# The first norm of a decoder layer by tokens, x turned on TensorE, and three of sixteen blocks of each first-projection row in plain float32

## The chip, the cores and the metric

The kernel runs one decoder layer on one core of one Trainium2 chip. Its time is the device time in microseconds (us) of one launch. The profile splits that core into TensorE (PE, with its weight loads PEld), VectorE (DVE), ScalarE (ACT), GpSimd (POOL) and SyncE (SP), which issues most of the transfers.

## The reference, cut to what matters

```python
def rmsnorm(x, g):
    xf = x.astype(F32)
    y = xf * lax.rsqrt(jnp.mean(xf * xf, axis=-1, keepdims=True) + EPS)
    return (y * g.astype(F32)).astype(x.dtype)

c_act = jax.nn.silu(c)
mod = (c_act @ w_ada[l] + b_ada[l]).reshape(B, 6, 1, D)
shift1, scale1, gate1, shift2, scale2, gate2 = jnp.moveaxis(mod, 1, 0)
h = rmsnorm(x, g_norm_mix[l]) * (1.0 + scale1) + shift1
q_a, k_c, v_c, k_s, v_s, k_w, v_w, g_a, q_r, k_r, v_r, g_r = split_cols(h @ w_in[l], IN_SIZES)
... attention and retention on these, the output projection, a second norm, the PEER layer ...
```

There are 256 tokens and 2048 features; everything is float32. `w_in` has 6704 columns. The change touches the norm of `x` and the first part of `h @ w_in`.

## The kernel before, in words

**Layout.** Features lie on the 128 partitions: `xT` holds x as 16 feature blocks k of [128 features x 256 tokens]. The projection `h @ w_in` is done in stages, each a stretch of the profile. Stage A (about 20 to 90 us) takes the blocks k = 0 to 7 of h against 2048 columns of `w_in` (16 output blocks of 128), one weight chunk `winA[k]` of 128 x 2048 (1 MB) for each k; this is "row k" below. Stage C takes the same k against 1024 more columns, stage B all 16 k against 1664 columns, stage D and later stages the rest, mixed with the attention. After them come the output projection, the second norm and the PEER layer, from about 700 us to the end.

**Splitting.** A float32 product is made of three products in the faster rounded type fp32r: each weight chunk is split by `split` into `whi` (a cast on ACT, line 157, in two halves) and `wlo` (raw minus whi on DVE, line 158, in two halves), and h into `hh` and `hl` in the tile `act`. `rows_T` (line 354) then issues hi x hh, hi x hl and lo x hh for each of the 16 blocks of a row: 48 matmuls of 256 columns.

**The modulation.** Scale and shift come from `w_ada`, 1 MB for each group of 128 outputs. `ada_chunk` loads one chunk and multiplies it by the row `crow` (silu of c) on DVE with a sum over the row (line 198). Row k of stage A needs two such chunks; with them `scol` and the shift of block k are made (lines 338 and 339, DVE), and `modulate` (lines 295 to 297) scales `xT[:, k]` in place on ACT, casts it to `hh` on ACT and subtracts to `hl` on DVE.

**The first norm before.** `xT` is loaded already turned by the host. Sixteen squares on ACT are added up by sixteen steps on DVE; `row_rstd` sums over partitions on PE, takes the power -0.5 on POOL, spreads the result over the partitions with one more matmul, and `normalise` multiplies all of `xT` by it on DVE (line 300).

**Buffers and queues.** Raw chunks (weights, w_ada, at the start also c) share a ring of four buffers `raw`; a load is issued on SP in the program's order as soon as the buffer's last reader is done, so a load that waits holds back all that stand behind it. Slot for slot, the chunk `winA[k]` hands its buffer to the first w_ada chunk of row k + 2. Each engine works through its own list in order; a scheduler that plans with its own model of times writes these lists when the program is built, so an edit can change the order of instructions that it doesn't name. `whi` and `wlo` have two buffers each. The eight PSUM banks go by the tags S, T, O and A, two each.

## Time and profile before

| what | value |
|---|---|
| three timed runs | 1860.74 us median, 1860.2 to 1863.67 us |
| profiled execution | 1856.91 us |
| its span, first to last instruction | 1855.2 us, mean granted clock 0.99 |
| busy share of the span | PE 97%, DVE 80%, ACT 38%, POOL 20% |
| HBM | 350 GB/s over the span |

The profiled execution's own time is 1.7 us above its span and 3.8 us below the median of the timed runs. A row of the timeline has the start, the duration, the engine, the line of the code, the operation, output and inputs, the shapes, the count, and in brackets how long the engine stood idle before it and what ended that. A row of the windows has the stretch and its length, then for each engine the busy time and the number of instructions, then the granted TensorE clock, the busy share of the DMA engines and the rate in GB/s. In the chain of waits a row has the start, the duration and what the end of the program hung on there.

### The profile page before, as it was taken

The numbers are of one execution on the slowest core, as the hardware profiler recorded it, in microseconds if no ns is written. First come the engines' busy times: TensorE is split into PE (matmuls) and PEld (weight loads), VectorE is DVE, ScalarE is ACT, GpSimd is POOL, SyncE is SP. The second block draws the span as 40 slices with busy tenths as digits, with TensorE's granted clock in tenths as the row PEclk, the third lists the DMA queues.
The fourth block names the chain that finished last, engine by engine and source line by source line (L and its number), as shares of the span: only waits on it lengthen the run. The fifth ranks groups of instructions, "written<-read, shape, count | busy, mean of one in ns | idle before, by whom it ended". The sixth has DMA issues, their size and how long they took to land.

```text
span 1855.2 us, 28510 instructions
## 1 busy us (share of the span) xinstructions
PE 1793.1 (97%) x11264; PEld 1571.5 (85%) x11264; DVE 1485.7 (80%) x2336; ACT 708.7 (38%) x1284; POOL 366.1 (20%) x259
## 2 busy tenths in 40 slices
PE   5899999999889999999999999999999999999997
PEld 4899878797767899999997777779999998777775
DVE  7988889889779999586498999983555558998878
ACT  3444453745435421021045555541111114555554
POOL 1000001011010012211124434420111114544210
PEclk9999899999999999999999999999999999999999
DMA  8989887889887799999889999989999989999992
GB/s 341 409 320 362 313 308 292 342 302 334 318 338 279 278 322 364 424 366 376 332 346 386 423 420 416 409 355 425 367 345 359 354 316 404 426 421 403 388 316 99
DMA packets 94616, 653.96 MB, mean 353 GB/s; under 512 B 11409, under 2 KB 11633, under 8 KB 18449
## 3 DMA queue, kind: packets, MB, share of 16 engines
q1 hardware_dynamic: 66818, 467.78, 65.2%
q0 software_dynamic: 27664, 184.37, 25.3%
q8 instruction: 88, 1.44, 0.3%
q14 instruction: 46, 0.38, 0.1%
HBM read 644.97 MB, written 4.22 MB: 350 GB/s over the span
## 4 chain that ended last, share of the span: by engine, by line
PE 87%; DVE 7%; DMA 3%; issue 1%; ACT 1%; POOL 0%; SPq 0%; ACTq 0%; POOLq 0%; DVEq 0%
PE acc L990 31%; PE psU L1111 28%; PE psN L453 8%; PE psD L354 4%; PE psA L237 3%; PE bkB L354 2%; DMA raw<-in_adaT 2%; PE psA L238 1%; PE pg L1096 1%; DVE raw L198 1%; DVE wlo L158 1%; PE bkC L354 1%; PE bvB L406 1%; DMA raw<-in_winA 1%; PE pT L552 1%
## 5 line engine op out<-in xcount | busy, mean ns | idle before, releaser
L1111 PE MATMUL psU<-xT,raw 128*128 128x160 f32 x4096 | 569.5, 300 | 0.0
L1111 PEld LDWEIGHTS psU<-xT,raw 128*128 128x128 f32 x4096 | 558.3, 190 | 0.4
L990 PE MATMUL acc<-whi,cc 128*128 128x512 f32 x1512 | 369.1, 391 | 0.0
L990 PEld LDWEIGHTS acc<-whi,cc 128*128 128x128 f32 x1512 | 283.8, 188 | 70.0 <-issue 1.5
L967 DVE TENSOR_TENSOR wlo<-raw,whi 128x2048 fp32r<-128x2048 f32 x126 | 288.1, 2287 | 55.1 <-issue 47.4
L990 PE MATMUL acc<-wlo,cc 128*128 128x512 f32 x1008 | 254.2, 392 | 0.8 <-DVE wlo L967 0.6
L964 ACT CAST whi<-raw 128x2048 fp32r<-128x2048 f32 x126 | 240.7, 1911 | 0.5 <-DMA raw<-in_v 0.5
L198 DVE SCALAR_TENSOR_TENSOR raw<-raw,crow 128x2048 f32<-128x2048 f32 x96 | 219.0, 2283 | 19.7 <-DMA raw<-in_adaT 19.6
L157 ACT CAST whi<-raw 128x1024 fp32r<-128x1024 f32 (+1 forms) x174 | 168.5, 1018 | 167.1 <-DMA raw<-in_winA 32.4
L158 DVE TENSOR_TENSOR wlo<-raw,whi 128x1024 fp32r<-128x1024 f32 (+1 forms) x174 | 200.6, 1181 | 24.2 <-ACT whi L157 23.8
L990 PEld LDWEIGHTS acc<-wlo,cc 128*128 128x128 f32 x1008 | 161.5, 161 | 63.8 <-DVE wlo L967 3.1
L453 PE MATMUL psN<-whi,act 128*128 128x512 f32 x512 | 166.9, 402 | 1.4 <-ACT act L677 0.7
L1117 DVE TENSOR_TENSOR X<-X,ge 128x160 f32<-128x160 f32 (+19 forms) x94 | 25.8, 276 | 162.7 <-ACT ge L1116 160.5
L1113 ACT ACTIVATE X<-psU 128x160 f32<-128x160 f32 (+19 forms) x102 | 25.6, 251 | 315.6 <-PE psU L1111 299.6
L453 PEld LDWEIGHTS psN<-whi,act 128*128 128x128 f32 x512 | 95.9, 189 | 25.6 <-issue 1.7
L453 PE MATMUL psN<-wlo,act 128*128 128x512 f32 x256 | 103.3, 404 | 3.4 <-DVE wlo L158 3.4
L953 ACT CAST cc<-X 128x192 fp32r<-128x192 f32 x126 | 44.0, 352 | 148.1 <-PE acc L990 147.5
L237 PE MATMUL psA<-act,whi 128*128 128x512 f32 x240 | 87.2, 404 | 3.8 <-ACT whi L157 3.8
L806 POOL DMA_INDIRECT rows<-in_urow,sx x32 | 67.1, 2097 | 105.3 <-DVE rows L847 100.4
L806 POOL DMA_INDIRECT s<-in_urow,sx x26 | 53.9, 2072 | 120.6 <-DVE s L847 86.5
L354 PE MATMUL psD<-act,whi 128*128 128x256 f32 x384 | 75.4, 294 | 0.6 <-ACT whi L157 0.6
L969 ACT CAST cc<-cc 128x64 fp32r<-128x64 f32 x126 | 30.4, 243 | 117.2 <-DVE cc L954 117.2
(363 smaller groups left out, 2551.0 us busy)
## 6 DMA issues: line engine op xcount, KB each, us to landing
raw<-in_u SPq DMA_DIRECT2D x128, 1024.0 KB
raw<-in_v SPq DMA_DIRECT2D x128, 1024.0 KB
raw<-in_adaT SPq DMA_DIRECT2D x96, 1024.0 KB
raw<-in_winN SPq DMA_DIRECT2D x16, 1024.0 KB
raw<-in_woutN SPq DMA_DIRECT2D x16, 1024.0 KB
raw<-in_wqT SPq DMA_DIRECT2D x16, 1024.0 KB
raw<-in_winB SPq DMA_DIRECT2D x16, 832.0 KB
raw<-in_winD SPq DMA_DIRECT2D x12, 1024.0 KB
```

The source lines that it names most:

```text
L157: nc.scalar.copy(hi[:, sl], r[:, sl])
L158: nc.vector.tensor_sub(lo[:, sl], r[:, sl], hi[:, sl].bitcast(F32))
L198: nc.vector.scalar_tensor_tensor(r, r, 1.0, crow, op0=OP.mult, op1=OP.mult, accum_out=modc[:, j, k:k + 1])
L237: nc.tensor.matmul(p_, hi[:, sl], act[:, k], start=k == 0, stop=False, skip_group_check=True)
L354: nc.tensor.matmul(bank[:, b, :], x[:, w], y[:, k, :], start=k == k0 and n == 0 and first, stop=k == k1 - 1 and n == 2, skip_group_check=True)
L453: nc.tensor.matmul(ps[tt], x[:, k, ts_], y[:, w], start=k == 0 and j == 0, stop=k == KB - 1 and j == 2)
L806: pin(nc.gpsimd.indirect_dma_start(out=r, out_offset=None, in_=src, in_offset=bass.IndirectOffsetOnAxis(ap=o, axis=0)))
L953: inorder(nc.scalar.copy(ch, xb(j)))
L964: inorder(nc.scalar.copy(hi, r))
L967: nc.vector.tensor_sub(lo[:, i:i + n], r[:, i:i + n], hi[:, i:i + n].bitcast(F32))
L990: return nc.tensor.matmul(acc[c][0:m], x, w[:, c[1] * 512:(c[1] + 1) * 512], start=jj == 0 and n == 0, stop=jj == HALF - 1 and n == 2 - c[ ...
L1111: nc.tensor.matmul(ps, w[:, k * P:(k + 1) * P], xT[:, k, 0:TU], start=k == 0, stop=k == KB - 1)
```

## The change

x is loaded by tokens, `xt` = [128 tokens, 2 halves, 2048], in four pieces. Four squares on ACT, each with its own sum over 1024 features, give the sums of squares directly (`ss0`); `token_rstd` makes the factor of each token (DVE, the power on POOL). The factors are put on the diagonal of two matrices (`dg00` and `dg01`), and 32 float32 matmuls of `xt` against them turn and scale x at once; each matmul is two records in the trace. ACT copies the results from eight PSUM banks to `xT`, 512 columns a time. `sumsq`, `row_rstd`, `normalise` and the host's turned copy of x go away.

In stage A the first NF = 3 of the 16 blocks of a row are multiplied in plain float32, straight from the raw chunk against the modulated `xT`; only the other 1664 columns are split. The raw buffer is thus read by PE too.

Lastly, the first four loads of `nal` (the distance penalties of the attention, on POOL's queue) now wait for a one-column copy from `gT`, which is made at the end of stage B; before, they were issued in the first microseconds.

```diff
-    o["xT"] = g["x"].reshape(S, KB, P).transpose(2, 1, 0)
...
-        for q in range(4):
-            nc.sync.dma_start(xT[:, 4 * q:4 * q + 4, :], a["xT"][:, 4 * q:4 * q + 4, :])
+        xt = fp.tile([P, 2, D], F32, name="xt", tag="oT")
+        for tt in range(2):
+            for h in range(2):
+                nc.sync.dma_start(xt[:, tt, h * 1024:(h + 1) * 1024], a["x"][:, tt, h * 1024:(h + 1) * 1024])
...
-        acc = fp.tile([P, S], F32, name="sqacc")
-        for k in range(KB):
-            sumsq(fp, k, acc, xT[:, k, :])
-        rrow = row_rstd(pp, fp, [acc], ["S", "S"], ident)
-        for k in range(0, KB, 4):
-            normalise(xT[:, k:k + 4, :], xT[:, k:k + 4, :], rrow)
+        ss = fp.tile([P, 2, 2], F32, name="ss0")
+        sq = fp.tile([P, 1024], F32, name="sq0", tag="cT")
+        for tt in range(2):
+            for h in range(2):
+                nc.scalar.activation(sq, xt[:, tt, h * 1024:(h + 1) * 1024], AF.Square, accum_out=ss[:, tt, h:h + 1])
+        rc = token_rstd(fp, ss, 2, "rc0")
+        dgs = []
+        for tt in range(2):
+            dgs.append(fp.tile([P, P], F32, name=f"dg0{tt}", tag=f"ksw{tt}"))
+            nc.vector.tensor_scalar(dgs[tt], ident, rc[:, tt:tt + 1], None, op0=OP.mult)
+        for k, t in zip(range(0, KB, 2), "SSTTOOAA"):
+            ps = pp.tile([P, 2, 2, P], F32, name="psx", tag=t)
+            for i in range(2):
+                for tt in range(2):
+                    nc.tensor.matmul(ps[:, i, tt, :], xt[:, tt, (k + i) * P:(k + i + 1) * P], dgs[tt], start=True, stop=True)
+            nc.scalar.copy(xT[:, k:k + 2, :], ps.rearrange("p i t s -> p i (t s)"))
...
         for k in range(KH):
-            hi, lo = win_row(a["winA"], k, 2048)
+            r = raw_tile()
+            nc.sync.dma_start(r, a["winA"][k])
+            hi, lo = split(r[:, NF * P:], 2048 - NF * P)
             row_in(k)
             background("A")
-            for b in range(16):
-                rows_T(bk[b // 2], b % 2, hi, lo, b * P, k, 0, KH, b % 2 == 0)
+            for b in range(NF):
+                nc.tensor.matmul(bk[b // 2][:, b % 2, :], r[:, b * P:(b + 1) * P], xT[:, k, :], start=k == 0 and b % 2 == 0,
+                                 stop=k == KH - 1, skip_group_check=True)
+            for b in range(NF, 16):
+                rows_T(bk[b // 2], b % 2, hi, lo, (b - NF) * P, k, 0, KH, b % 2 == 0)
...
                     nal = fp.tile([P, 384], F32, name="nal", bufs=4)
+                    if gp == 0 and r < 2:
+                        nc.scalar.copy(nal[:, 0:1], gT[:, 0:1])
                     nc.gpsimd.dma_start(nal, a["nali"][h])
```

The order of the loads on SP in stage A is the same as before: two w_ada chunks, one `winA` chunk, and again. On ACT and DVE the order changes. Line numbers of the changed kernel are other ones: its lines 264, 265 and 266 are the lines 295, 296 and 297 of before (the modulation), 156 and 157 are 157 and 158 (the split), 197 is 198 (w_ada times c), 314 and 315 are 338 and 339, 347 and 349 are 370 and 372 (the copies of stage A's results out of PSUM, on DVE and on ACT).

On ACT, in stage A, two rows k and k + 1 read so before:

```order
L157 CAST whi<-raw 128x1024 x2
L295 ACTIVATE xT<-xT,modc,scol 128x256
L296 CAST act<-xT 128x256
L157 CAST whi<-raw 128x1024 x2
L295 ACTIVATE xT<-xT,modc,scol 128x256
L296 CAST act<-xT 128x256
```

and in the changed kernel so:

```order
L264 ACTIVATE xT<-xT,modc,scol 128x256
L156 CAST whi<-raw 128x832 x2
L265 CAST act<-xT 128x256
L264 ACTIVATE xT<-xT,modc,scol 128x256
L156 CAST whi<-raw 128x832 x2
L265 CAST act<-xT 128x256
```

The cast of a row's weight chunk stood ahead of the row's modulation (which waits for `scol`); it now stands behind it.

On DVE, in stage A of the changed kernel, one row and the head of the next read:

```order
L197 SCALAR_TENSOR_TENSOR raw,modc<-raw,crow 128x2048 x2
L314 TENSOR_TENSOR modc<-modc,cols 128x2
L315 TENSOR_SCALAR scol<-modc,cols 128x1
L157 TENSOR_TENSOR wlo<-raw,whi 128x832 x2
L266 TENSOR_TENSOR act<-xT,act 128x256
L197 SCALAR_TENSOR_TENSOR raw,modc<-raw,crow 128x2048 x2
```

`scol` is followed at once by the subtraction `wlo`, which needs the cast; before, the second subtraction (L297, `act`) stood between the two w_ada multiplies instead of ahead of them.

At the turn from stage A to stage C, ACT reads before:

```order
L372 COPY oT<-bkA_192 128x512
L372 COPY oT<-bkA_194 128x512
L157 CAST whi<-raw 128x1024 x2
L372 COPY oT<-bkA_196 128x512
L295 ACTIVATE xT<-xT,modc,scol 128x256
L372 COPY oT<-bkA_198 128x512
```

and in the changed kernel the first cast of stage C stands behind all four copies:

```order
L349 COPY oT<-bkA_187 128x512
L349 COPY oT<-bkA_189 128x512
L349 COPY oT<-bkA_191 128x512
L349 COPY oT<-bkA_193 128x512
L156 CAST whi<-raw 128x1024 x4
```

On DVE at the same turn, the changed kernel has both w_ada multiplies behind the last subtraction of stage A (L266) and ahead of stage C's first `wlo`; before, one of the two stood ahead of that subtraction:

```order
L266 TENSOR_TENSOR act<-xT,act 128x256
L197 SCALAR_TENSOR_TENSOR raw,modc<-raw,crow 128x2048
L347 COPY oT<-bkA_188 128x512
L347 COPY oT<-bkA_190 128x512
L197 SCALAR_TENSOR_TENSOR raw,modc<-raw,crow 128x2048
L347 COPY oT<-bkA_192 128x512
L347 COPY oT<-bkA_194 128x512
L314 TENSOR_TENSOR modc<-modc,cols 128x2
L157 TENSOR_TENSOR wlo<-raw,whi 128x1024
```

In the attention (from about 200 us on) the lists of PE, DVE and ACT hold the same work in partly other order.

More of the change, by code (lines that the diff above doesn't have):

```diff
@@ L247, in summed @@
         nc.vector.tensor_add(dst, dst, ps[:, 0, 0:n])
-    def sumsq(wpool, kb, acc, src, tag="pr"):
-        sq = wpool.tile([P, S], F32, name="sq", tag=tag, bufs=3)
-        nc.scalar.activation(sq, src, AF.Square)
-        if kb == 0:
-            nc.vector.tensor_copy(acc, sq)
-        else:
-            nc.vector.tensor_add(acc, acc, sq)
-    def row_rstd(pool, wpool, accs, tags, ident, copy=True):
-        ps = [pool.tile([P, 2], F32, name="psq", tag=t) for t in tags]
-        for i, acc in enumerate(accs):
-            for tt in range(2):
-                nc.tensor.matmul(ps[tt][:, 0:1], acc[:, tt * P:(tt + 1) * P], ones[:, 0:1], start=i == 0, stop=i == len(accs) - 1)
-        rc = wpool.tile([P, 2], F32, name="rcol")
-        for tt in range(2):
-            nc.vector.tensor_scalar(rc[:, tt:tt + 1], ps[tt][:, 0:1], 1.0 / D, EPS, op0=OP.mult, op1=OP.add)
-        pow_mhalf(rc, rc, 2)
-        dg = wpool.tile([P, S], F32, name="rdiag", tag="pr", bufs=3)
-        for tt in range(2):
-            nc.vector.tensor_scalar(dg[:, tt * P:(tt + 1) * P], ident, rc[:, tt:tt + 1], None, op0=OP.mult)
-        ps = pool.tile([P, S], F32, name="psr", tag=tags[0])
-        nc.tensor.matmul(ps, ones, dg, start=True, stop=True)
-        if not copy:
-            return ps
-        r = wpool.tile([P, S], F32, name="rrow")
-        nc.scalar.copy(r, ps)
-        return r
     with ExitStack() as fctx:
@@ L297, in modulate @@
             nc.vector.tensor_sub(hl[:, k:e, :], t, hh[:, k:e, :].bitcast(F32))
-        def normalise(dst, src, rrow):
-            nc.vector.tensor_mul(dst, src, rrow[:, None, :].to_broadcast([P, dst.shape[1], S]))
         kcv = fp.tile([P, 4, 2, P], F32, name="kcv", tag="f4k", bufs=2)
-        ksw = [fp.tile([P, S], F32, name=f"ksw{i}") for i in range(4)]
         vsw = fp.tile([P, 2, 512], F32, name="vsw")
         gT = fp.tile([P, S], F32, name="gT", tag="pr", bufs=3)
-        oT = fp.tile([P, KB, S], F32, name="oT")
-        cT = fp.tile([P, KB // 2, S], F32, name="cT")
         pp = fctx.enter_context(tc.tile_pool(name="fpsum", bufs=2, space=PS))
@@ L312, in body @@
         crow = c_row(fp, pp)
-        for q in range(4):
-            nc.sync.dma_start(xT[:, 4 * q:4 * q + 4, :], a["xT"][:, 4 * q:4 * q + 4, :])
+        xt = fp.tile([P, 2, D], F32, name="xt", tag="oT")
+        for tt in range(2):
+            for h in range(2):
+                nc.sync.dma_start(xt[:, tt, h * 1024:(h + 1) * 1024], a["x"][:, tt, h * 1024:(h + 1) * 1024])
         rowc = dram.tile([1, D], F32, name="rowc")
         nc.gpsimd.dma_start(rowc, crow[0:1, :])
-        acc = fp.tile([P, S], F32, name="sqacc")
-        for k in range(KB):
-            sumsq(fp, k, acc, xT[:, k, :])
-        rrow = row_rstd(pp, fp, [acc], ["S", "S"], ident)
-        for k in range(0, KB, 4):
-            normalise(xT[:, k:k + 4, :], xT[:, k:k + 4, :], rrow)
+        ss = fp.tile([P, 2, 2], F32, name="ss0")
[14 more added lines that the diff above has]
+            nc.scalar.copy(xT[:, k:k + 2, :], ps.rearrange("p i t s -> p i (t s)"))
+        ksw = [fp.tile([P, S], F32, name=f"ksw{i}") for i in range(4)]
+        oT = fp.tile([P, KB, S], F32, name="oT")
+        cT = fp.tile([P, KB // 2, S], F32, name="cT")
         todo = [(j, k) for k in range(KB) for j in (1, 0)] + [(j, k) for j in (2, 4, 3) for k in range(KB)] + [(5, k) for k in range(LATE)]
@@ L360, in body @@
         KH = KB // 2
+        NF = 3
         def row_in(k):
```

## The prediction

> **What bounds the kernel now.** I read the page's chain of waits first, then the chain in order of time and the windows for the stretch that the change touches, then the timelines of DVE, ACT and PE there.
>
> ```profile
> PE 87%; DVE 7%; DMA 3%; issue 1%; ACT 1%; POOL 0%; SPq 0%; ACTq 0%; POOLq 0%; DVEq 0%
> ...
> 41.09 7.33 DMA raw<-in_winA
> ...
> 72.23 7.27 DMA raw<-in_winA
> ...
> 85.62 5.00 PE bkA L354 x40
> 90.62 22.77 PE bkC L354 x192
> ...
> 60.00:80.00 20.00, 16.40 (x122) 15.78 (x121) 19.57 (x25) 6.24 (x9) 0.00 (x0) 0.91 1.00 409
> 100.00:120.00 20.00, 20.00 (x164) 19.64 (x163) 15.36 (x19) 9.12 (x12) 0.00 (x0) 1.00 0.85 296
> ```
>
> Over the whole run PE sets the end. Stage A is the exception: until 85.62 us the chain hangs on loads of `winA` and on DVE. In 60 to 80 us the DMA engines are at 1.00 and 409 GB/s, DVE is busy 19.57 of 20 us, and PE only 16.40. From 90.62 us on PE is full, so what the change does to the time is the moment at which stage C can run, and whatever the changed order does later. A matmul saved or added inside stage A is hidden.
>
> One row of stage A before, on ACT and DVE:
>
> ```profile
> 71.43 1.99 ACT L157 CAST whi<-raw 128x1024 fp32r<-128x1024 f32 x2 [4.49 <-DMA raw<-in_winA]
> 72.43 0.21 DVE L339 TENSOR_SCALAR scol<-modc,cols 128x1 f32<-128x1 f32 x1
> 72.56 2.35 DVE L158 TENSOR_TENSOR wlo<-raw,whi 128x1024 fp32r<-128x1024 f32 x2
> 73.33 0.60 ACT L295 ACTIVATE xT<-xT,modc,scol 128x256 f32<-128x256 f32 x1
> 74.83 2.28 DVE L198 SCALAR_TENSOR_TENSOR raw<-raw,crow 128x2048 f32<-128x2048 f32 x1
> 77.04 0.42 DVE L297 TENSOR_TENSOR act<-xT,act 128x256 fp32r<-128x256 f32 x1
> 77.38 2.28 DVE L198 SCALAR_TENSOR_TENSOR raw<-raw,crow 128x2048 f32<-128x2048 f32 x1
> 79.91 0.21 DVE L339 TENSOR_SCALAR scol<-modc,cols 128x1 f32<-128x1 f32 x1
> ...
> 38.64 0.21 DVE L339 TENSOR_SCALAR scol<-modc,cols 128x1 f32<-128x1 f32 x1
> 38.89 0.60 ACT L295 ACTIVATE xT<-xT,modc,scol 128x256 f32<-128x256 f32 x1 [8.89 <-DVE scol L339]
> ...
> 91.41 0.33 PE L354 MATMUL bkC<-act,wlo 128*128 128x256 f32 x1
> ```
>
> The cast of row 6 starts when its chunk lands (71.43), a microsecond ahead of `scol` of row 6 (72.43), so DVE goes from `scol` into `wlo` without a pause. A row takes 79.91 - 72.43 = 7.48 us here; from the load at 41.09 to that at 72.23 four rows take 31.14, so 7.8 for a row and 2.6 us for each of its three 1 MB chunks. `scol` of row 1 is at 38.64, that of row 7 at 79.91, and stage C's first matmul with a `wlo` at 91.41: these three are what I move.
>
> **The change part by part.**
>
> *The start.* Rows that go away, or give prices:
>
> ```profile
> L255 DVE TENSOR_TENSOR sqacc<-sqacc,sq 128x256 f32<-128x256 f32 x15 | 6.4, 424 | 1.5 <-ACT sq L251 0.2
> L300 DVE TENSOR_TENSOR xT<-xT,rrow 128x1024 f32<-128x1024 f32 x4 | 4.6, 1219 | 0.0
> L537 POOL DMA_DIRECT2D nal<-in_nali x4 | 2.1, 560 | 0.0
> ...
> 12.84 1.33 ACT L251 ACTIVATE sq<-xT 128x256 f32<-128x256 f32 x4 [0.67 <-DMA xT<-in_xT]
> 15.70 2.29 DVE L198 SCALAR_TENSOR_TENSOR raw<-raw,crow 128x2048 f32<-128x2048 f32 x1 [1.45 <-DMA raw<-in_adaT]
> 20.61 1.99 ACT L157 CAST whi<-raw 128x1024 fp32r<-128x1024 f32 x2 [6.44 <-DMA raw<-in_winA]
> 21.37 0.71 POOL L221 TENSOR_TENSOR rcol<-rcol,mhalf 128x2 f32<-128x2 f32 x1 [8.67 <-DVE modc L338]
> 22.12 0.48 DVE L269 TENSOR_SCALAR rdiag<-small,rcol 128x128 f32<-128x128 f32 x2 [0.58 <-POOL rcol L221]
> ```
>
> DVE loses 6.4 + 4.6 = 11.0 us of work ahead of row 1. The four `nal` loads (128 x 384 float32 each, 0.75 MB together, 1.95 us at 2.6 us for a MB) no longer share the engines with x: x is there at 12.84 - 1.95 = 10.9, the first w_ada chunk at 13.75, the second at 16.35, `winA[0]` at 18.7 (as late as before, if the share of `nal` was nothing). Four squares of 1024 columns cost about 4 x 0.33 = 1.3 us each by the row at 12.84; the last ends at 12.2. Sum and scaling on DVE, the power (0.71) and the two diagonals (0.48) end at 13.9. Then DVE multiplies w_ada chunks, 2.21 us each (74.83 to 77.04): 16.1 and 18.6, `scol` of row 0 at 18.9. The first copy of turned x, the modulation and the two casts of row 0 go by on ACT until 21.7, `wlo` ends at 22.9; two more w_ada chunks and one subtraction follow (25.1, 25.4, 27.6), and **`scol` of row 1 stands at 27.9**, 10.7 us earlier than 38.64. Bounds: 27.0 (casts right as the chunk lands) to 29.6 (every load as late as before).
>
> *The turn of x on PE.* 64 records. Float32 against 128 columns isn't in the trace; the nearest rows are 60 columns below and 160 above:
>
> ```profile
> 196.71 3.67 PE L487 MATMUL psc<-blk,raw 128*128 128x60 f32 x32
> 1256.86 30.51 PE psU L1111 x224
> ...
> 27.13 2.07 PE L354 MATMUL bkA<-act,whi 128*128 128x256 f32 x8 [3.25 <-ACT act L296]
> 39.98 1.21 PE L354 MATMUL bkA<-act,whi 128*128 128x256 f32 x8 [0.70 <-ACT act L296]
> ```
>
> 3.67 / 32 = 0.115 and 30.51 / 224 = 0.136 us for a record; I take 0.12, so 7.7 us. The same eight matmuls took 2.07 us at 27.13 and 1.21 at 39.98: PE starts slow. I take twice the price for the first 5 us from 13.9 (some 21 records, just the first bank's share in the written order) and 0.12 for the rest: the turn ends at about 24, ACT's copies at 25.5. Bounds: 21.6 (never slow) to 29.3 (always). Row 0's float32 matmuls follow, and only then is the buffer of `winA[0]` free, at 26.0.
>
> *A row of stage A.* 832 columns instead of 1024 in each half of the split, and the order shown above:
>
> ```profile
> 107.64 1.68 ACT L157 CAST whi<-raw 128x832 fp32r<-128x832 f32 x2 [3.68 <-DVE raw L198]
> 108.56 1.96 DVE L158 TENSOR_TENSOR wlo<-raw,whi 128x832 fp32r<-128x832 f32 x2 [0.50 <-ACT whi L157]
> ```
>
> From `scol` on: 0.25 until ACT starts the modulation (38.64 to 38.89), 0.60 for it, 0.84 for the first half of the cast (1.68 / 2), 0.1 to pass the result: `wlo` starts at 1.8, where before it started at 0.13. So DVE saves 2.35 - 1.96 = 0.4 us of work and gains 1.67 us of waiting. Then 1.96 for `wlo`, 0.34 for the subtraction, 2 x 2.21 for w_ada, 0.32 to the next `scol`: **8.8 us a row** (bounds 8.6 to 9.0), against 7.8 of DMA work, so the loads get ahead and no longer bind. Row 7's `scol` is at 27.9 + 6 x 8.8 = 80.7, against 79.91.
>
> PE in a row: three plain blocks instead of nine products. By the 160-column row, 2 x 0.136 x 256 / 160 = 0.44 us each, 1.3 in all; nine products by stage C's row (22.77 / 192 = 0.119) 1.07. The 0.25 us more is hidden by PE's waits for DVE, whose longest is 2.8 us:
>
> ```profile
> PE bkA L354 <- DVE act L297: 10.0, 6, 2.8
> ```
>
> If that cover went, eight rows would cost 2 us.
>
> *The turn to stage C.* On ACT the first cast of C waits for all four copies, on DVE `wlo` waits for both w_ada chunks and four copies. From row 7's `scol`: 4.1 to the end of the subtraction, 2.21, two copies of about 0.6, 2.21, two copies, 0.1, then `wlo` 1.1, and 0.1 to pass it: 12.2 us. Stage C's first `wlo` matmul is at 92.9. The row before is 91.41: **1.5 us later**, of an early gain of 10.7. By the bounds of `scol` of row 1, 0.6 to 3.2.
>
> *PE's clock.* With that order PE pauses about 1 us behind stage A and some 2 us more for `wlo`. In the trace one of four such pauses of 1.5 to 1.8 us was followed by a lower clock:
>
> ```profile
> 70.04 0.39 PE L354 MATMUL bkA<-act,whi 128*128 128x256 f32 x1 [1.84 <-DVE act L297]
> ...
> 70.00:74.00 4.00, 3.96 (x23) 3.96 (x24) 3.93 (x6) 2.54 (x4) 0.00 (x0) 0.66 0.97 379
> ```
>
> 4 us at 0.66 cost 1.4; I add a quarter, 0.4. The Trainium skill, "TensorE: Matmul & The Clock Gate", Part 1, has the clock halve only after an idle window of about 3.4 us. By that rule the term would be nothing and the sum 0.4 less; the row at 70 us, behind a pause of 1.84, does not agree with it.
>
> *`nal` and the rest.* The four loads now issue when `gT` is copied, behind stage B. Their first reader is far behind:
>
> ```profile
> 216.10 0.29 DVE L546 CUSTOM_DVE_ANT_0 pr<-sc,nal 128x128 f32<-128x128 f32 x1
> ...
> 468.20 4.87 DMA raw<-in_adaT
> ...
> 400.00:500.00 100.00, 93.28 (x486) 77.64 (x485) 85.39 (x129) 47.41 (x74) 14.95 (x13) 0.98 0.89 325
> 500.00:600.00 100.00, 90.53 (x443) 74.12 (x442) 84.87 (x138) 45.82 (x77) 8.27 (x14) 0.93 0.83 310
> ```
>
> Stage B ends near 187 us, a 1 MB load into a quiet queue takes 4.87 us, so some 20 us of cover remain; without it, up to 5 us. In the attention the lists are reordered. PE is idle there only 100 - 93.28 + 100 - 90.53 = 16.2 us in 400 to 600; the reorder may move a quarter of it either way, -4 to +4. I take +0.5, since stage D's two groups of compressed keys now stand side by side on PE and the second waits for DVE.
>
> **Sum:** 1.5 + 0.4 + 0.5 = 2.4 us. The span of 1855.2 becomes 1857.6, the profiled execution 1859.3 instead of 1856.9. The median of the timed runs lies 3.8 above the profiled execution; added to it, 1860.7 + 2.4 = **1863.1 us**.
>
> **The rivals.** Within 0.2% (3.7 us) counts as no change, about what a measurement of this kernel can tell.
>
> *Faster: the wait for ACT costs nothing, and rows stay at 7.8 us.* For it: DMA at 1.00 in 60 to 80 us, and DVE has less work. It needs `scol` not to be the last to come, that is, chunks that land later than the modulation. Against it: with 8.8 us on DVE there are 1.0 us of DMA to spare in each row. Price: 6 x 1.0 less, 2.4 - 6.0 = -3.6, and up to -5 with the early bound of `scol`: about 1856.5 us.
>
> *Slower: a slow PE holds the ring at the start.* The fifth w_ada chunk, row 2's first, goes into the buffer of `winA[0]`, which PE's float32 matmuls release, behind the turn of x. It is needed 4.1 us after `scol` of row 1, at 32.0, and takes 4.87: the buffer must be free by 27.1, and I have it at 26.0. If PE stays slow through the turn, copies and row 0's float32 matmuls push the release to some 30, the chunk to 35, and rows 2 on by 2.7 to 3 us; all loads behind it on SP wait too. Price: 2.4 + 2.9, about 1866 us. Against it: PE was at full speed 5 us after the start of row 0 before. It decides from a turn that ends later than 25.
>
> *The attention's new order outweighs the front*, by up to 4 us to either side, 1859 or 1867. Nothing in the order speaks for a side.
>
> **How the numbers follow.** My case (stage C 0.6 to 3.2 us later) 0.47, faster rival 0.19, slower rival 0.26, attention 0.08 in halves. My case alone spans 1860 to 1864.4. The range takes in the faster rival's 1856.5 and ends at 1867.5 above the slower one. Faster by over 0.2%: 0.19 + 0.03 = 0.22. Slower: 0.26 + 0.04 = 0.30. Within: 0.48.
>
> **What would show it.** `scol` of row 1 near 28 us; rows of 8.8 us with some 1.6 us of DVE waiting for ACT's `whi` in each, and a DMA share below 0.95 in 40 to 80 us; stage C's first `wlo` matmul near 93. Wrong, if rows take under 8.2 us, if the fifth w_ada chunk is waited for, or if the same stretch of 190 to 700 us is more than 3 us longer or shorter.

## The result and the profile after

The changed kernel takes **1870.28 us** (median of 10 runs, 1867.23 to 1876.09) against 1860.06 us (10 runs, 1857.44 to 1864.34) of the kernel before in the same session: ratio **1.0053, 95% interval 1.0043 to 1.0063**. It is slower by some 10 us, where 1863.1 was forecast and the range ended at 1867.5. The profiled execution took 1867.77 us with a span of 1866.0, against 1855.2 before; the mean granted clock is 0.99 in both.

The front of the kernel went as forecast. The timeline of the changed kernel, ACT, DVE and PE in stage A and at the turn to stage C:

```profile
24.84 1.56 PE L360 MATMUL bkA<-xT,raw 128*128 128x256 f32 x6
25.01 0.33 SPq L147 DMA_DIRECT2D raw<-in_adaT  x1
27.76 0.21 DVE L315 TENSOR_SCALAR scol<-modc,cols 128x1 f32<-128x1 f32 x1
...
70.79 0.21 DVE L315 TENSOR_SCALAR scol<-modc,cols 128x1 f32<-128x1 f32 x1
71.04 0.60 ACT L264 ACTIVATE xT<-xT,modc,scol 128x256 f32<-128x256 f32 x1 [6.14 <-DVE scol L315]
71.55 1.65 ACT L156 CAST whi<-raw 128x832 fp32r<-128x832 f32 x2
72.45 1.96 DVE L157 TENSOR_TENSOR wlo<-raw,whi 128x832 fp32r<-128x832 f32 x2 [1.44 <-ACT whi L156]
79.40 0.21 DVE L315 TENSOR_SCALAR scol<-modc,cols 128x1 f32<-128x1 f32 x1
...
91.42 0.39 PE L330 MATMUL bkC<-act,wlo 128*128 128x256 f32 x1 [1.74 <-DVE wlo L157]
```

`scol` of row 1 is at 27.76 (forecast 27.9), that of row 6 at 70.79 and that of row 7 at 79.40: 8.61 us a row, with the pause of 1.44 us on DVE for ACT's cast that the order on ACT foretold. Stage C's first matmul with a `wlo` is at 91.42, where before it was at 91.41. `scol` of row 1 was 10.9 us earlier than before (27.76 against 38.64); all of that is gone by then, and nothing is lost.

So the front isn't where the time went. The milestones of the two profiled executions (us; each is the start of the first or of the last matmul of a group on PE):

| milestone | before | after | later by |
|---|---|---|---|
| stage C, first `wlo` matmul | 91.4 | 91.4 | 0.0 |
| stage B ends | 185.8 | 185.9 | 0.1 |
| stage D (`psD`, with the attention) ends | 418.3 | 418.9 | 0.6 |
| last matmul of the retention (`por`) | 459.0 | 463.4 | 4.4 |
| last stage and output projection (`psN`) end | 544.7 | 552.6 | 7.9 |
| queries of the PEER layer (`psA`) begin | 561.6 | 570.6 | 9.0 |
| first expert products (`psU`) begin | 662.0 | 671.1 | 9.1 |
| `psU` ends | 1544.0 | 1553.2 | 9.2 |
| end of the last products (`acc`) | 1844.0 | 1854.8 | 10.8 |

7.3 of the 10.8 us show between 419 and 553 us. The change doesn't edit one instruction there. The windows of the changed kernel (columns as before: PE, PEld, DVE, ACT, POOL, then the clock, the DMA share, GB/s):

```profile
60.00:80.00 20.00, 15.03 (x104) 13.02 (x103) 16.52 (x22) 5.29 (x9) 0.00 (x0) 1.00 1.00 377
...
400.00:500.00 100.00, 91.57 (x484) 76.24 (x483) 85.64 (x139) 45.70 (x71) 14.96 (x12) 0.97 0.84 315
500.00:600.00 100.00, 89.39 (x420) 71.39 (x419) 81.95 (x119) 44.84 (x77) 8.35 (x14) 0.93 0.83 301
```

PE was busy 93.28 and 90.53 us in the last two before. The finer windows of PE alone (stretch, length, PE busy, clock, DMA share, GB/s) show the place; first the kernel before, then the changed one:

```profile
419.00:440.00 21.00, 19.08 (x92) 1.00 0.98 349
440.00:460.00 20.00, 20.00 (x95) 1.00 0.91 351
```

```profile
419.00:440.00 21.00, 21.00 (x107) 1.00 0.89 334
440.00:460.00 20.00, 15.57 (x67) 0.91 0.97 373
```

In 440 to 460 us, PE was full at full clock before and issued 95 matmuls; now it is busy 15.57 us at a clock of 0.91 and issues 67. What it waits for is the retention's last part: `por` (the retention's output, line 636) for ACT's normalisation of an earlier head (`orr`, line 651), and the transposes of it for DVE's gate (line 656). The timeline of PE, of before and then of the changed kernel:

```profile
458.46 0.38 PE L652 MATMUL por<-vr,at 128*128 128x128 f32 x2
```

```profile
449.03 0.79 PE L636 MATMUL por<-vr,at 128*128 128x128 f32 x2 [3.50 <-ACT orr L651]
...
452.76 0.74 PE L498 MATMUL psT<-small,orr 128*128 128x128 f32 x4 [0.80 <-DVE orr L656]
...
557.74 2.64 PE L720 MATMUL psX<-small,xn 128*128 128x128 f32 x10 [4.76 <-DVE xn L715]
```

Before, the `por` groups behind stage D ran without a wait, 0.38 us for two records, and the one shown, the last, has the long `psN` matmuls on both sides. Now the third of them has a wait of 3.50 us ahead of it and the slower clock behind it (0.79 for two records). Before, 24 of the 48 `por` records had been done by the end of stage D, now 12, so that more of this chain stands behind 419.

Two smaller pieces: the gap from `psN` to `psA` (the second norm) is 18.0 us instead of 16.9, and at the very end the clock fell once:

```profile
1834.00:1844.00 10.00, 7.96 (x24) 4.47 (x23) 7.83 (x8) 2.23 (x5) 0.00 (x0) 0.83 0.01 2
```

Before, the two stretches of 10 us from 1824 to 1844 were at 1.00. The last two rows of the table differ by 1.6 us of the 10.8, and these belong to this one profiled execution.

### The profile page after: what moved, and what is told of

Same layout as the page of the kernel before. It is cut to its first block, busy times and chain, and to the rows that moved or that the text cites. A ratio compares the mean times of both kernels' runs of the same rounds, so it can differ in the third digit from the quotient of the medians.

```text
span 1866.0 us, 28592 instructions
## 1 busy us (share of the span) xinstructions
PE 1807.7 (97%) x11298; PEld 1577.9 (85%) x11298; DVE 1471.6 (79%) x2316; ACT 707.7 (38%) x1285; POOL 366.0 (20%) x259
## 4 chain that ended last, share of the span: by engine, by line
PE 79%; DVE 11%; DMA 5%; issue 3%; ACT 1%; POOL 0%; SPq 0%; ACTq 0%; POOLq 0%; DVEq 0%
PE acc L974 30%; PE psU L1095 28%; DMA raw<-in_adaT 4%; PE psN L435 3%; DVE raw L197 3%; PE psA L236 3%; DVE wlo L157 2%; PE bkB L330 2%; PE psD L330 2%; PE psA L237 1%; PE pg L1080 1%; PE bvB L388 1%; PE bkC L330 1%; PE sc L526 1%; PE pT L536 1%
## 5 line engine op out<-in xcount | busy, mean ns | idle before, releaser
L157 DVE TENSOR_TENSOR wlo<-raw,whi 128x1024 fp32r<-128x1024 f32 (+1 forms) x174 | 197.6, 1162 | 28.2 <-ACT whi L156 27.9
L790 POOL DMA_INDIRECT rows<-in_v,sx x25 | 64.0, 2558 | 56.9 <-DVE sp L837 30.6
```

The costliest lines, as they stand in the source:

```text
L157: nc.vector.tensor_sub(lo[:, sl], r[:, sl], hi[:, sl].bitcast(F32))
L790: pin(nc.gpsimd.indirect_dma_start(out=r, out_offset=None, in_=src, in_offset=bass.IndirectOffsetOnAxis(ap=o, axis=0)))
```

## The experiments

My theory after the result: **the order of the instructions from stage D on costs the time**; it was rewritten by the scheduler because of the wait on the first four `nal` loads. Rival one: the front (its loads, its clock, the float32 blocks) or the late landing of the held `nal` loads leaves something behind that shows only later. Rival two: a single wait in the new order (ACT's `orr`, a late load, DVE's w_ada multiplies), which could be taken out by itself.

Several kernels have the order of one kernel's lists forced on another. At the end of the build, each engine's list gets an edge from every instruction to the next; such an edge sets the order of issue and adds no wait:

```diff
+        i = L[-k]
+        if prev is not None:
+            tc.add_manual_dep(i, prev.name, dep, reason="pin_tail")
+        prev = i
```

### Which part of the change costs it

**The change with the order of before.** From stage D's first matmul on, the lists of PE, DVE, ACT and SP are those of before; the front and the wait on `nal` stay.

> The changed kernel whole, its hold of nal included, but from the first matmul of stage D on (about 188 us) the lists of PE, DVE, ACT and SP are forced into the order that they have in the kernel before; POOL's list and everything ahead of 188 us stay as changed. Theory 1, the new order of the later stages costs the time: 1860 to 1862.5 us, with the output projection's last matmul near 546 us as in the kernel before (544.7), not at 552.6. Theory 2, the four nal loads cost it by landing late and in the way: 1868 to 1871. Theory 3, what the change does ahead of 188 us costs it (something there is late for the later stages though stage B ends at the same moment): 1868 to 1871.

Measured: 1859.17 us, ratio to before 1.0007 (0.9993 to 1.0021). The whole loss is gone with the order. What is left of the change, the front and the late `nal` loads, is worth nothing that this interval can tell from zero.

**The reverse: before with the changed kernel's order** from stage D on.

> The kernel before, nothing of the change in it (old norm, old rows, nal loads at the start), but from the first matmul of stage D on the lists of PE, DVE, ACT and SP are forced into the order of the changed kernel. Theory 1 (the new order alone costs the time): 1867 to 1872 us, with a wait of PE of 3 to 5 us for the normalisation of the retention near 445 to 456 us. Theory 2 (the nal loads that land late, which the forced old order only hid): 1858 to 1861. Theory 3 (front): 1858 to 1861.

Measured: 1868.64 us, 1.0039 (1.0024 to 1.0055). The order alone, with the old front and the `nal` loads at the start, costs most of it. Its timeline of PE has the same wait at the same place:

```profile
450.91 0.79 PE L654 MATMUL por<-vr,at 128*128 128x128 f32 x2 [3.53 <-ACT orr L669]
```

**Before with the hold alone**, the two lines and nothing else:

```diff
+                    if gp == 0 and r < 2:
+                        nc.scalar.copy(nal[:, 0:1], gT[:, 0:1])
```

> The kernel before, with the old norm and the old rows of stage A, and only the first four nal loads held back by a one-column copy from gT. Its lists from stage D on then read as in the changed kernel. Theory 1 (order): 1867 to 1871 us, though norm and rows are the old ones, with a wait of PE of about 3.5 us near 445 to 449 us. Theory 2 (late loads): 1867 to 1871 as well. Theory 3 (front): 1859 to 1861.5.

Measured: 1871.86 us, 1.0065 (1.0045 to 1.0086). With these two lines the scheduler writes, from stage D on, the lists of the changed kernel, instruction for instruction; and the time is lost, even 12 us of it (8 to 16 by the interval). So the order comes from the hold, not from the norm and not from the float32 blocks.

**The norm alone**, 16 split blocks a row and no hold. From stage D on its lists are those of before.

> Only the first norm by tokens with x turned on TensorE; stage A's rows with all 16 blocks split, nal not held. The lists from stage D on read as in the kernel before, and on ACT the cast of most rows stands ahead of the modulation again. Theory 1: the loss is gone and so is the wait of 1.67 us a row for ACT: rows of 7.8 us by their loads, scol of row 1 near 28 and of row 7 near 75 us (79.9 before, 79.4 in the change), stage C's first matmul with wlo near 87 (91.4 in both), so 4 to 5 us faster than before: 1854 to 1857. Theory 3 (the start on PE and the early rows cost it): 1863 or more.

Measured: 1859.84 us, 0.9997 (0.9982 to 1.0013). This is a miss for me: I had expected a gain of 3 to 6 us. `scol` of row 1 was at 30.07, and row 7's at 78.05, 1.9 us ahead of before. ACT's timeline says why no more:

```profile
77.78 2.00 ACT L156 CAST whi<-raw 128x1024 fp32r<-128x1024 f32 x2 [5.22 <-DMA raw<-in_winA]
```

The last chunk of `winA` lands at 77.7 us, whatever DVE and ACT have gained. Stage A's end is bound by the loads, and those were nearly full before.

**The change without the hold.**

> The changed kernel with the nal loads not held. Stage A's lists stay as in the change; the lists of the later stages are a third order, neither that of before nor that of the change. Theory 1: the front is worth what it was in the change, about nothing at 188 us, and the third order decides: 1856 to 1866, with the place of the difference again between 190 and 560 us. Theory 2 (late loads): 1860 to 1862. Theory 3: 1868 to 1871.

Measured: 1862.87 us, 1.0018 (1.0004 to 1.0031). Here the scheduler wrote a third order, neither that of before nor that of the change, and the time lies between the two. The float32 blocks without the hold shift the lists too, though otherwise.

### Which piece of the order

**The old order in stage D, the new one behind 419 us.**

> The changed kernel with the order of before forced from the first matmul of stage D to its last (about 188 to 419 us), and the order of the change behind it. It tells in which half of the new order the loss sits. If it is lost in the projections of 188 to 419 us, because a pair of retention heads less is done there: 1859 to 1862. If it is lost in the output projection and the second norm behind 419 us: 1866 to 1870. If half and half: 1862 to 1866.

Measured: 1870.75 us, 1.0052 (1.0031 to 1.0072). No gain at all, though the retention's part is done early again. PE waited 10.9 us behind stage D, and the wait for `orr` was 4.08 us:

```profile
451.53 0.80 PE L639 MATMUL por<-vr,at 128*128 128x128 f32 x2 [4.08 <-ACT orr L654]
```

So the loss is there with the old order in stage D too. How it divides between the two halves isn't shown by this run, since the old lists in stage D and the new ones behind it make a mixture with waits of its own. (In the profile, stage D itself got a lower clock, 0.74 in 200 to 220 us, and ended 3.8 us later than in the changed kernel.)

**Moving single links of the waiting chain**, in the changed kernel's order. In the first, the normalisation's factors on DVE and `orr` on ACT are moved ahead in their lists; in the second, the factors are constants; in the third, the last piece of x for the second norm is loaded later on SP, behind the fourth chunk of the output projection; in the fourth, the factors, `orr` and DVE's two gate multiplies are moved ahead together, on DVE and ACT.

> The changed kernel in its own order, with one place mended: on DVE the two brs of the retention pair at 443 us stand right behind their bmv (437 us) and the two bnb right behind the w_ada multiply of 439 us, and on ACT the four normalisations orr stand ahead of the cast of whi of 446 us. If PE's wait of 3.5 us there, and the lower clock behind it (0.93 and 0.90 in 440 to 460 us, 1.7 us), are what the order costs: 1863 to 1866, with no wait of PE over 1 us in 440 to 456. If the wait only moves to the next place: 1867 to 1870.

> The changed kernel in its own order (forced from stage D on), with the normalisation of the retention reading a constant column for scale and bias instead of the factors brs and bnb (so the retention is left unnormalised; every instruction stays and costs the same, only ACT no longer waits for DVE and POOL there). Theory (behind 419 us the new order pays because PE's next por waits for this chain: 3.50 us at 449, 4.08 in the run with the old head): that wait goes and 4 to 7 us come back, 1863 to 1866. Rival (the wait moves on to the next link, as it did when the factors were made earlier: 5.98 us for the gate's multiply): 1868 to 1871.

> The changed kernel in its own order (forced from stage D on), with one load moved on SP: the last of the eight pieces of x (256 KB, into the space of xT), which waits there until the last score of the retention (scr) has read that space, goes behind the fourth woutN chunk instead of ahead of the first. In every run with the new order that load issues right behind the last scr, at 432 to 442 us, and the first woutN within 0.4 to 0.9 us behind it; in the old order the load is at 424.7 and the woutN at 430.1. Theory (the retention, a pair of heads later in the new order, holds all woutN loads through that one load, and ACT's cast of the late chunk holds the retention's orr and the gate behind it): the first woutN issues 2 to 5 us earlier, PE's waits of 3.5 and 0.8 us at 449 and 453 fall below 1 in sum, and 3 to 7 us come back: 1863 to 1867. Rival (the chunk is held by its buffer anyway, or the waits move on once more): 1868 to 1871.

> As the run with the factors early (brs, bnb and orr moved ahead), and on DVE the two gate multiplies orr of the same heads also moved, from behind the w_ada multiplies of 449 and 453 us to ahead of them, behind the first wlo of 446 us. In that run the wait of PE had moved to them: 5.98 us at 456. Theory (behind 419 us the new order costs because a whole chain of small steps of a pair of heads stands behind w_ada multiplies of 2.3 us and casts on DVE and ACT, so that each link moved alone only hands the wait on): with all its links ahead, PE's waits in 440 to 460 us fall below 2 us and 4 to 7 us come back against the new order: 1863 to 1866. Rival (the loads of woutN and the w_ada chunks, at a share of 0.97 to 0.99 in 440 to 460 us, bind whatever the order of the small steps): 1868 to 1871.

Measured, in this order: 1870.98 us, 1.0049 (1.0033 to 1.0066); 1871.03, 1.0060 (1.0043 to 1.0076); 1869.27, 1.0046 (1.0032 to 1.0060); 1872.59, 1.0067 (1.0047 to 1.0087). None gave anything back. The waits of PE that stood in the place of the 3.50 us; one fence for each kernel in the same order:

```profile
456.01 1.09 PE L501 MATMUL psT<-small,orr 128*128 128x128 f32 x4 [5.98 <-DVE orr L659]
```

```profile
453.19 0.80 PE L639 MATMUL por<-vr,at 128*128 128x128 f32 x2 [3.50 <-ACT orr L654]
```

```profile
452.15 0.79 PE L639 MATMUL por<-vr,at 128*128 128x128 f32 x2 [3.40 <-ACT orr L654]
```

```profile
460.02 0.50 PE L438 MATMUL psN<-whi,act 128*128 128x512 f32 x1 [3.05 <-ACT sg L620]
...
470.67 0.49 PE L639 MATMUL por<-vr,at 128*128 128x128 f32 x2 [1.98 <-ACT orr L654]
```

With the factors early the wait went to the next link (DVE's gate multiply, which then stood behind two w_ada multiplies, 5.98 us); with constant factors and with the later load it stayed; with all these links early it split into several. For this wait, rival two, a single wait that can be taken out, falls with these four.

**DVE's w_ada multiplies made short.** In the next kernels 18 w_ada multiplies behind 419 us work on 256 of 2048 columns, 18 times 0.42 us instead of 2.28; once with the full loads, in the new and in the old order, and once with loads of 256 columns too:

```diff
-        nc.vector.scalar_tensor_tensor(r, r, 1.0, crow, op0=OP.mult, op1=OP.mult, accum_out=modc[:, j, k:k + 1])
+        n = 256 if (j == 3 and k >= 4) or (j == 5 and k < LATE) else D
+        nc.vector.scalar_tensor_tensor(r[:, 0:n], r[:, 0:n], 1.0, crow[:, 0:n], op0=OP.mult, op1=OP.mult, accum_out=modc[:, j, k:k + 1])
```

> The changed kernel in its own order (forced from stage D on), with the 18 w_ada multiplies that DVE does behind 419 us shortened from 2048 to 256 columns, so that they take some 0.4 us instead of 2.3 (all loads and all waits stay; the second norm's shift and part of the last gate are then sums over 256 columns only). Order theory, sharpened: in the new order the retention's small steps stand on a DVE that is busy 15.00 of 15 us in 415 to 430 and in 430 to 445, and come late. Then this gives back what the order costs: 1859 to 1864 us, with PE's wait of 3.50 us at 449 gone or below 1. Rival: the new order costs by its loads (a DMA share of 0.96 to 0.98 in 440 to 460) or by PE's own work left over at 419 us: 1866 to 1870, with waits as before.

> The same shortening in the changed kernel with the order of before: the control. If DVE binds only where the new order has left it more to do: 1857 to 1860, with the waits at 424 and 487 us, which end with a chunk's landing, shorter by at most the 1.9 us that each multiply loses. If DVE binds this stretch in any order, it gains as much as the new order does: 1851 to 1855.

> The changed kernel in its own order (forced from stage D on), with the 18 w_ada chunks that are used behind 419 us both multiplied and loaded for 256 of their 2048 columns only (128 KB a load instead of 1 MB; the second norm's shift and part of the last gate are sums over 256 columns). With the multiplies alone shortened the new order took 1865.6 us and the old one 1854.3. Theory (loads: in 440 to 460 us their share is 0.96 to 0.99 and the casts of woutN wait for landings): the new order comes within 3 us of the old one with the same cut, both at 1848 to 1856. Rival (the lists themselves): some 10 us stay between the two, the new order at 1859 to 1864.

> The same cut in the changed kernel with the old order: the control. Theory (loads): 1848 to 1853, 1 to 3 us from the new order with the cut. Rival (lists): 1849 to 1854, some 10 us below the new order with the cut.

Measured: new order 1865.63 us, 1.0029 (1.0018 to 1.0040), old order 1854.29, 0.9966 (0.9956 to 0.9976); with short loads new order 1865.37, 1.0023 (1.0011 to 1.0035), old order 1856.1, 0.9977 (0.9965 to 0.9989). Less work on DVE helps both orders, by 0.0024 to 0.0041 (4 to 8 us), and the distance between the orders stays: 11 and 9 us. The new order's 1865.63 lies between its theory and its rival, its 1865.37 above both. Neither these multiplies nor these loads carry the distance. The wait for `orr` stays too, in the two kernels with the new order:

```profile
451.68 0.49 PE L640 MATMUL por<-vr,at 128*128 128x128 f32 x2 [2.89 <-ACT orr L655]
```

```profile
452.59 0.80 PE L646 MATMUL por<-vr,at 128*128 128x128 f32 x2 [2.79 <-ACT orr L661]
```

**w_ada multiplies moved later in the old order**, to see whether that order can still be bettered by the same means.

> The changed kernel with the order of before from stage D on, as in the first run, and two w_ada multiplies on DVE moved: the one that waits for its chunk until 484 us stands behind the two wlo of the next weight chunk, the one at 421 us behind the addition to xT. In the kernel before PE waits 3.42 us for that wlo (487.75) and 1.92 us for that xT (423.76), and the clock is 0.88 and 0.95 in 480 to 500 us (1.7 us). If these waits set the end: 4 to 6 us less than the first run, 1853 to 1856, and faster than both kernels. If the w_ada chunks that are then issued later become the bound: 1858 to 1860.

Measured: 1860.61 us, 1.0001 (0.9987 to 1.0014). No gain; the wait I had aimed at went elsewhere:

```profile
481.56 0.50 PE L438 MATMUL psN<-wlo,act 128*128 128x512 f32 x1 [2.47 <-DVE wlo L160]
```

### What the order does in stage D: score tiles side by side

A score tile `sc` of the attention is a product over 64 features. It takes 64 of PE's 128 rows: the lower half of the partitions for one head, the upper for the other (`hs = slice(hf * 64, hf * 64 + 64)`). In the program's order the halves come as lower, lower, upper, upper, and so on. If the lists take the tiles in pairs, a pair has one half; shifted by one tile, a pair has both. The timeline of PE, with 64*128 as the part of PE that an instruction takes; two neighbouring tiles in the changed kernel:

```profile
286.34 0.49 PE L525 MATMUL sc<-ksw,xT 64*128 64x128 f32 x2
286.66 0.59 PE L526 MATMUL sc<-ksw,xT 64*128 64x256 f32 x2
287.10 0.38 PE L525 MATMUL sc<-ksw,xT 64*128 64x128 f32 x2
287.32 0.59 PE L526 MATMUL sc<-ksw,xT 64*128 64x256 f32 x2
287.84 0.55 PE L576 MATMUL pcT<-small,ppad 128*128 128x128 f32 x3
```

and two neighbours in the kernel before:

```profile
344.64 0.50 PE L541 MATMUL sc<-ksw,xT 64*128 64x128 f32 x4
344.96 0.61 PE L542 MATMUL sc<-ksw,xT 64*128 64x256 f32 x4
345.50 0.50 PE L453 MATMUL psN<-whi,act 128*128 128x512 f32 x1
```

Both are eight records. In the first, on one half, they take 287.84 - 286.34 = 1.50 us; in the second, on opposite halves, 345.50 - 344.64 = 0.86: the two tiles run at the same time. A tile with other products on both sides takes 0.85 us from its start to the next product's, so the second of such a pair costs next to nothing. The order of before has four such pairs, the new order none whole. The windows of stage D for the tile `sc` alone (PE busy, clock, DMA share, GB/s), of before, of the changed kernel and of before with the new order:

```profile
188.00:420.00 232.00, 27.20 (x128) 0.98 0.83 309
```

```profile
188.00:420.00 232.00, 31.02 (x128) 0.99 0.84 307
```

```profile
188.00:420.00 232.00, 31.02 (x128) 0.98 0.83 304
```

128 records each, 3.8 us apart, by the order. From start to start on PE, `sc` has 24.8 us of stage D before and 28.3 in the changed kernel, the transposes `pT` 12.1 and 13.1, `poc` 3.1 and 3.4: 4.8 us in all. Stage D is yet not longer, since PE leaves retention work undone in exchange (`por`, `scr` and transposes, some 2.5 us), and since its first 12 us had the full clock, where before they had 0.86. Part of what shows behind 419 is thus work that stage D left. From `psD`'s first matmul to the end of `psN` the changed kernel takes 7.8 us longer (364.5 against 356.7): PE's idle time grows by 2.9 of them (8.6 to 11.5), `sc` and `pT` by 4.5, `por` by 2.0, smaller groups by some 2, and `psD` takes 3.7 less.

To test the pairs by themselves I took the change with the old order, with one improvement in stage A (ACT's cast forced ahead of the modulation, as it stood before):

```diff
+                if after is not None:
+                    tc.add_manual_dep(m.ins, after.ins.name, mybir.DependencyInfo(mybir.DependencyClass.NoSync, mybir.DependencyReason.DATA), reason="cast first")
...
-            row_in(k)
+            row_in(k, lastcast[0])
```

> The changed kernel with the order of before from stage D on and, in stage A, the cast of a row's weights forced ahead of the modulation on ACT, as in the kernel before; nothing else. The step under test: rows take 8.6 us because the cast stands behind the modulation. If so, DVE's wait for whi (1.6 us a row) goes, rows fall to the 7.8 us of their three loads, scol of row 7 stands at 77 to 78.5 instead of 79.4 (the last winA chunk lands at 77.7 in the run with the norm alone), stage C's first wlo matmul at 89.5 to 90.5 instead of 91.4, and the time is 0 to 2 us below the run with the old order alone: 1857 to 1859.5. If rows stay at 8.6: the same time as that run.

Measured: 1856.88 us, 0.9981 (0.9965 to 0.9998). Stage C's first `wlo` matmul is at 89.63 instead of 91.42. The timelines of DVE and PE:

```profile
27.14 0.21 DVE L322 TENSOR_SCALAR scol<-modc,cols 128x1 f32<-128x1 f32 x1
...
77.34 0.21 DVE L322 TENSOR_SCALAR scol<-modc,cols 128x1 f32<-128x1 f32 x1
...
89.63 0.39 PE L337 MATMUL bkC<-act,wlo 128*128 128x256 f32 x1 [0.20 <-DVE wlo L162]
```

A row takes (77.34 - 27.14) / 6 = 8.4 us, where I had expected 7.8. Now the loads set it: the cast of row 6 has 4.81 us of waiting for `winA` in front of it. So the cast's place did cost the 1.8 us at the turn; more isn't to be had there, since the loads are the next bound.

On this kernel I then made eight more pairs of opposite halves, by the order on PE and the other lists alone; and, from the same kernel, broke up the four that there are.

> The change with the cast forced first in stage A and the order of before from stage D on, and in PE's list eight pairs of score tiles sc brought side by side, one tile on the lower and one on the upper 64 rows of PE; the matmuls that stood between go ahead of them or behind. Four such pairs stand side by side in the order of before, none whole in the order of the change. In the traces so far the 128 records of sc, start to next start, sum to 24.7 to 24.8 us in the old order and 28.3 in the new, and eight records in a row take 0.86 us when the tiles lie on opposite halves but 1.50 when on the same half. Theory (tiles on opposite halves run at the same time): each new pair gives back 0.6 to 0.8 us, sc sums to 18.5 to 20 us and the time falls by 3 to 6 us below the 1856.9 of the cast-first run, to 1851 to 1854. Rival (what is gained on PE is lost in waits for the score tiles' buffers, or the rows only look shorter): 1856 to 1858.

> The same kernel, cast first and old order, with the four pairs that stand side by side in the order of before broken up: two matmuls of psN (once one of pT and one of psN) between the tiles. Theory (opposite halves run at the same time): sc sums to some 27.5 us instead of 24.7 and the time is 2 to 3.5 us above the cast-first run: 1859 to 1860.5. Rival: no difference, 1856 to 1858.

Measured: with twelve pairs 1850.5 us, 0.9950 (0.9932 to 0.9968); with none 1860.49, 1.0008 (0.9996 to 1.0021). The two ran side by side: 10.0 us for twelve pairs, 0.83 us a pair. Against the kernel that they were made from, by the ratios, it is 0.0031 (5.8 us) less for eight pairs more, and 0.0027 (5.0 us) more for four pairs fewer, each with an interval of 0.002 to 0.0025 to either side. The windows of tile `sc`, of twelve pairs, then of none:

```profile
188.00:420.00 232.00, 19.12 (x128) 0.98 0.88 326
```

```profile
188.00:420.00 232.00, 30.82 (x128) 0.98 0.83 307
```

From start to start `sc` sums to 17.6 and 28.1 us in the two profiled executions, 10.5 us apart; `pT` differs by another 1.6. The time follows the pairs in both directions, and the twelve pairs make a kernel that beats both kernels of this study, by some 9 us the one before and by some 19 the changed one, by the ratios; 3.5 of these came with the cast put first.

## Why the prediction was wrong

**The step that failed** is the term "*nal* and the rest", taken as +0.5 us with bounds of -4 and +4. It measured +7 to +9: 1.0053 for the change against 1.0007 with the old order is 8.6 us, and the order alone put on the kernel before costs 1.0039, or 7.3. The reason given for the +0.5 held (the second group of compressed keys waited 2.35 us for DVE, 1.00 before), but it was a small part. The step had two faults. The bound was a quarter of PE's idle time in 400 to 600 us, as if an order could only move waits; but PE's busy time itself depends on which tiles stand side by side (3.5 us more for `sc` in the changed kernel; that pairs move the time is shown by making and breaking them), and a lower clock stood behind the new wait (0.91 in 440 to 460, 1.00 before). How much of the 7 to 9 us is the pairs' isn't shown: with the old order in stage D the four pairs were back, `sc` at 24.8 us, and the time was not. And the sentence "Nothing in the order speaks for a side" was not true: the phase of the `sc` tiles stood in the lists of both kernels, and in the trace of before eight records at 0.86 us stood beside others at 1.50. I had looked at the lists of PE only where two groups of compressed keys came together.

**The third rival** (the attention's new order outweighs the front, 1867) was the right case, with half the size and a chance of 0.04 (half of 0.08) for this side. The sign that the prediction named for being wrong, 190 to 700 us more than 3 us longer, is what happened: from `psD`'s start to `psU`'s start it is 473.6 us before and 482.6 now, 9.0 longer.

**The front's steps held.** `scol` of row 1: 27.76 for 27.9. Rows: 8.61 for 8.8, with a pause of 1.44 on DVE for the cast where 1.67 was worked out. Row 7: 79.40 for 80.7. The turn of x ended at 23.4 where I had 24; the buffer of `winA[0]` let the fifth w_ada chunk go at 25.01, ahead of the 27.1 at which the slow-PE rival would have begun. Stage C was forecast 1.5 us later and came 0.0 later; the rows, 0.2 us shorter each, make most of that. It lies outside the stated 0.6 to 3.2, which were worked out from the bounds of row 1 alone; the row's own 8.6 to 9.0, six times over, would have added 1.2 to either side. Eight float32 rows of PE stayed hidden, as said.

**The clock term** (+0.4) can't be judged by one execution. Behind the same pause at the turn, the changed kernel kept its clock in 92 to 96 us, and the change with the old order lost half of it; the windows of the one and of the other (all engines):

```profile
92.00:96.00 4.00, 4.00 (x36) 4.00 (x35) 4.00 (x4) 1.47 (x3) 0.00 (x0) 1.00 0.87 299
```

```profile
92.00:96.00 4.00, 4.00 (x20) 4.00 (x20) 4.00 (x4) 0.53 (x2) 0.00 (x0) 0.50 0.87 305
```

The second ended stage C 2.6 us later (115.8 against 113.2). A price of 2.6 with some chance was the right kind of term; a quarter of 1.4 was a low one.

**One sign was wrong**: a DMA share below 0.95 in 40 to 80 us. It is 0.97 in 40 to 60 and 1.00 in 60 to 80, though rows there wait for ACT and the engines move only 377 GB/s against 409 before. So the share didn't tell that there was room; the rate did.

**The faster rival** fell for the reason given (rows at 8.6). With the cast put first and the old order behind, its price comes out about as worked out, 1.9 thousandths or 3.5 us less than before against -3.6, though by another way than it said: rows take 8.4 us and not 7.8, and stage C begins 1.8 us earlier. With an interval of 0.0002 to 0.0035 the agreement isn't worth much.

**What stays open.** The order costs some 7 to 12 us; that is shown five times (8.6 with the old lists on the change, 7.3 with the new lists on before, 12 with the hold alone, 11 and 9 in the two pairs of kernels with short multiplies). That a pair is worth some 0.8 us is shown on the old order. That they are worth as much in the new order wasn't tried by itself, and the old order put back in stage D alone gave nothing, so the two pieces don't simply add up. Which property of the lists behind 419 us costs the rest isn't settled: the wait for `orr` is where it shows, but every way that I tried of taking it away or relieving it moved it or left it. PE's idle time there doesn't tell the orders apart either; the windows (all engines) of the kernel before and of the changed one:

```profile
419.00:546.00 127.00, 119.32 (x522) 94.72 (x520) 104.38 (x143) 56.40 (x84) 11.55 (x14) 0.99 0.89 329
```

```profile
419.00:546.00 127.00, 118.57 (x522) 94.06 (x521) 103.34 (x144) 59.74 (x92) 11.17 (x15) 0.97 0.85 314
```

That is 7.7 us idle before and 8.4 now. With the old order it is 4.8 in the change and 10.5 in the norm alone (a profiled execution 3.5 us above its median), and neither of these two kernels lost time.

## What to carry to other kernels

When a scheduler writes the lists, compare both kernels' lists over the whole program, also far behind the edit, and price what changed places: a two-line hold cost 12 us here by itself (8 to 16), and the order it brought 7 to 9, far behind the place of the edit's own work. To separate an edit from the order that comes with it, force the old order on the new kernel and the new order on the old one; that told more here than moving single instructions. And a wait that shows in the trace is where a loss is seen, not always what makes it: the same loss came out at `orr`, at the gate, at `psN`, as each in turn was moved.

## What the runs showed of the hardware

Two products over 64 rows on opposite halves of PE run at the same time if they are neighbours in PE's list: 0.86 us for eight records against 1.50 on one half and 0.85 for the four records of a tile alone, and 0.83 us off the kernel's time for each pair, over twelve pairs. The Trainium skill, "TensorEngine Tiling (Array Packing)", Tiling Modes, Key Properties, says it so: "Different tiles can execute LdWeights and Matmul in parallel". The trace agrees, with these numbers; the prediction hadn't drawn on it.

The same pause of 1.7 us was followed by a clock of 1.00 in one kernel and 0.50 in another, at the same place with the same matmuls. One thing in the traces tells the two apart. Their stretches of low clock are at 0.50 and last 3.41 us or a multiple of it, on a fixed grid in each execution (the last stretch of an execution aside). Two neighbouring windows of this grid, first in the change with the old order, then in the changed kernel (stretch, length, PE busy, clock, DMA share, GB/s):

```profile
87.06:90.47 3.41, 1.59 (x12) 1.00 1.07 387
90.47:93.88 3.41, 2.46 (x11) 0.50 0.89 303
```

```profile
86.71:90.12 3.41, 1.95 (x15) 1.00 0.98 329
90.12:93.53 3.41, 2.10 (x17) 1.00 0.88 348
```

The same two pauses, 1.0 and 1.7 us, fell otherwise on the grid: PE was busy 1.59 of 3.41 us (47%) in the one window and 1.95 (57%) in the other, and only the first was followed by the half clock. In the kernel before, 1.57 us busy in 67.84 to 71.25 stands ahead of the 0.50 from 71.25 on. Over the twenty traces, between 37 and 582 us, all 72 windows at full clock with PE busy under 45% were followed by one at 0.50, and of 2762 with PE busy over 70% only 9 were. The Trainium skill, "TensorE: Matmul & The Clock Gate", Part 1, has the clock decided over windows of about 3.4 us that run free of the kernel. The traces agree, with 3.41; that a window a little more than half idle is enough, as in these rows, isn't what that part says.
